# A two-layer decoder trunk on one core: weight differences, query-tile roots, paired transposes and halved loads are re-ordered

## The chip, the cores and the metric

The kernel runs on one core of a Trainium2 chip. The metric is the device time of one execution, in microseconds (us), as the median of several runs. A core has a matrix engine (TensorE; PE in the profile, with its weight loads shown apart as PEld), three elementwise engines (VectorE = DVE, ScalarE = ACT, GpSimd = POOL) and SyncE (SP), which here does little but issue DMA transfers, in the order of its queue. The engines run their own instruction streams in order and wait for each other by semaphores.

## The reference

The input is one sequence of 1024 positions of width 1024, all in 32-bit floats, with 256 memory tokens. There are two layers. Each normalises its input, multiplies it with one wide weight matrix, mixes the result over the positions, attends to the memory tokens, multiplies by a gate and projects back:

```python
for l in range(DEPTH):                       # 2
    h = rms_norm(x, norm_gain[l])
    cols = h @ w_in                          # mixer columns | memory queries | gate
    mix = dilated_mixer(...) if l % 2 == 0 else hgrn2_mixer(...)
    mem_out = memory_cross_attention(q_mem, mem, ...)
    y = concatenate([mix, mem_out]) * silu(gate)
    x = x + y @ w_out
```

The first layer's mixer has three groups of eight heads. Each group has its own q, k and v (1024 columns each), attends causally in a window of 128 keys gathered with a stride of 1, 4 or 16, with q and k normalised per head and rotated; the three outputs are merged per head by their softmax denominators. The second layer's mixer is a gated linear recurrence, done in chunks; its values are 1024 columns of the wide product.

## The kernel before

**Products in two parts.** A 32-bit product is made of three fast ones: each operand is split into a high part (a copy by ACT, `split_high`, `high_b`, written `h_` in the lists below) and a low part (the difference, by DVE, `split_low`, `low_b`, `l_`); PE adds high x high, high x low and low x high.

**Seven products instead of eight.** The nine q, k and v products of the first layer, and the v product of the second, are made in the 2 x 2 block scheme with seven block products, p = 0 to 6. The right-hand blocks of a product are raw weights (`11`, `21`, `12`, `22`, each in two halves of 512 KB) or differences of them, which `combine` makes on DVE: 12 - 11, 22 - 12, 22 - 11, 21 - 22. The products with p = 0 and 1 use the raw blocks 11 and 21. Each block product has four tiles, i = 0 to 3, and each tile is a step of twelve matmuls of 128 x 512. `step(k)` runs step k = 4 n + i of product n: the matmuls, then the emptying of the tile before, then `weights_ahead(n, i)`, which prepares the weights of the next block product: high parts at i = 0 and 1, low parts at i = 1 and 2, differences and loads by small tables. The variable `late` shifts the first three differences by one step; it is 0 in the first layer and 1 in the second.

**Tiles of q and k** of the first layer are normalised and rotated after their last product (DVE and POOL), then turned by PE six steps behind (`flip`, four 128 x 128 transposes into one bank of `pT`, which has two), copied out one step later by ACT (`spill_heads`) and stored to DRAM by a DMA on SP's queue (`qk_scr`). 96 such tiles are made, in runs of consecutive steps that start at an even step. After the last step the same function runs eight times more without matmuls, between matmuls for the memory tokens; two tiles of the memory are turned through `pT` there as well (`mem_turn`).

**The attention of the first layer** goes through twelve pairs (g, hp) of a group and two heads, in the order of `heads`, with eight steps m each. A step computes scores (L1537), turns an earlier step's weights (L1551), multiplies an earlier one with v (L1564, four steps after its scores), and fills PE with gate products while g is 2. After every second step the output goes through one of three `os` tiles to `o_scr` in DRAM, two stores of 128 KB; for g = 0 the three groups' outputs are merged instead, with the others loaded back (`og`). q, k and v of a pair, 1 MB each, are loaded ahead: `fetch_qk(at + 2)` at step 0, `fetch_v(at + 1)` at step 3. There are three rooms for q and k and two for v. For g = 1 these loads are already in two halves, for g = 0 and 2 each is one load. For g = 0, `fetch_v` also loads the statistics of the other groups. Only PE's order is written out here; a planner orders the other engines and SP's queue.

**The start of the second layer** has eight query tiles t (`project`, 24 matmuls each), whose matmuls hide other work: `slots[t]` lists the block sums of the 2 x 2 scheme for the left-hand side. `w_` adds high and low part to a whole block on POOL, `c_` combines blocks on DVE, `h_` and `l_` split them again. Beside them each step turns the query tile of two steps ago (L363), copies out the one of three steps ago (`spill_q`), and takes the root of the one before (`root_q`: a reduction and a scaling on DVE, a power on POOL, L1768 to L1770), then squares its own tile (`square_q`, two operations of ACT). Here PE, DVE, ACT and POOL all run in the order in which the code writes them (`pinned`). The seven-product scheme for v follows at once; the raw weights `21` (half 0) and `12` are loaded into room that the block sums leave.

Of the kernel before, what the change touches and what calls it, by code (L numbers as in the profile page):

```python
# [54 lines left out]
BEHIND = 6  # L55
# [48 lines left out]
def trunk_kernel(ctx, tc, x, mem, pos, norm_gain, w_in_a, q_gain_a, k_gain_a, qk_gain_t, w_out_a,  # L104
# [4 lines left out]
    LQ, SQ, WQ = Y, A, Y  # L109
# [689 lines left out]
    with ExitStack() as sa:  # L799
# [171 lines left out]
        def split_low(n, h):  # L971
            if n < 7 * len(groups):
                hi = highs.pop((n, h))
                lo = wpool.tile([128, 1024], F32R, name="wl")
                V.tensor_tensor(lo[:], source(n, h), hi.bitcast(F32), op=OP.subtract)  # L975
                split[n, h] = [t.rearrange("p (k n) -> p k n", k=2) for t in (hi, lo[:])]
# [4 lines left out]
        def weights_ahead(n, i):  # L981

            gi, p = divmod(n, 7)
            first, second = (1, 0) if p == 0 else (0, 1)
            sums_ = {(0, late): ("12", "12", "11", 0), (0, 1 + late): ("12", "12", "11", 1), (0, 2 + late): ("22", "22", "12", 0),
                     (1, 0): ("22", "22", "12", 1), (1, 3): ("11", "22", "11", 0), (2, 0): ("11", "22", "11", 1),
                     (2, 3): ("21", "21", "22", 0), (3, 0): ("21r", "21r", "22", 1)}
            if i in (0, 1):
                split_high(n + 1, (first, second)[i])
            if i in (1, 2):  # L990
                split_low(n + 1, (first, second)[i - 1])
            if (p, i) in sums_:
                out, a, b, h = sums_[p, i]
                combine(gi, out, a, b, h)
            for at, what in (((0, 2), ((0, "22", 1),)), ((2, 2), ((0, "21r", 1),)), ((2, 3), ((1, "11", 0),)),
                             ((3, 0), ((0, "22r", 0),)), ((3, 1), ((0, "22r", 1),)), ((4, 2), ((1, "11", 1),)),
                             ((4, 3), ((1, "12", 0), (1, "12", 1), (1, "21", 0))), ((5, 2), ((1, "22", 0),)),
                             ((5, 3), ((1, "21", 1),))):
                if at == (p, i):
                    for more_, b, h in what:  # L1000
                        load(gi + more_, b, h)
# [118 lines left out]
        late = 0  # L1120
# [4 lines left out]
        def step(k, fill=None):  # L1125

            n, i = divmod(k, 4)
            if k <= LAST and k not in sums_at:
                sums_at[k] = matmuls(k)
            spill_heads(k - 1 - BEHIND)  # L1130
            if k - 1 in sums_at:
                emptied(k - 1, sums_at.pop(k - 1))
            normed(k - 3)
            if k <= LAST:
                weights_ahead(n, i)
                if 3 < k < 26 and made_tables:
                    if next(tables, tables) is tables and made_tables:
                        made_tables.pop()()
                if i == 3 and n % 7 == 0 and groups[n // 7][0] != 2:
                    group_tables(*groups[n // 7])  # L1140
            if fill:
                fill()
            spread(k - 1)
            flip(k - BEHIND)

        wraws, W, gates = {}, {}, {}

# [233 lines left out]
        rooms_ = [None, None]  # L1381

        def fetch_qk(at):
            if at >= len(heads):
                return
            g, hp = heads[at]
            pool, n = (rooms_[1], 2) if at % 3 else (rooms_[0], 1)
            q, k = (pool.tile([128, 2, S], F32, name=name, bufs=n) for name in ("qT", "kT"))
            heads_at[g, hp] = q, k
            for i, t in ((1, k), (0, q)):  # L1390
                if g == 1:
                    src = qk_scr[i][g].rearrange("p h s -> p (h s)").rearrange("p (a h c) -> p a h c", a=2, c=512)
                    for a in range(2):
                        LQ.dma_start(t[:].rearrange("p h (a c) -> p a h c", a=2)[:, a], src[:, a, 2 * hp:2 * hp + 2])
                else:
                    LQ.dma_start(t[:], qk_scr[i][g][:, 2 * hp:2 * hp + 2])

        def fetch_v(at):
            if at >= len(heads):
                return  # L1400
            g, hp = heads[at]
            pool = rooms_[at % 2]
            v = pool.tile([128, NT, 256], F32, name="vv", bufs=1)
            src = v_scr[g][:, hp * 256:(hp + 1) * 256]
            if g == 0:
                LQ.dma_start(v[:], src.rearrange("(m p) c -> p m c", p=128))
            elif g == 1:
                src = src.rearrange("(a p b) c -> p a b c", a=2, b=4)
                for a in range(2):
                    LQ.dma_start(v[:, 4 * a:4 * a + 4], src[:, a])  # L1410
            else:
                LQ.dma_start(v[:], src.rearrange("(p m) c -> p m c", m=8))
            st = pool.tile([128, 128], F32, name="st", bufs=1)[:, 0:NG * NT * 4].rearrange("p (g m a h) -> p g m a h", g=NG, m=NT, a=2)
            if g == 0:
                for i in range(2):
                    LQ.dma_start(st[:, 1 + i].rearrange("p m a h -> p m (a h)"), st_scr[i, hp].rearrange("(m p) c -> p m c", p=128))
            heads_at[g, hp] += v, st

        def fetch(at):
            fetch_qk(at)  # L1420
            fetch_v(at)


        with ExitStack() as sm:
# [84 lines left out]
        if True:  # L1509
# [114 lines left out]

            fill = fillers()
            scored, turned, rest = [], [], []
            fetch_qk(1)
            for at, (g, hp) in enumerate(heads):
                for m in range(NT):
                    with pinned():  # L1630
                        new = (g, hp, m, *scores(g, hp, m))
# [13 lines left out]
                            {0: load_piece, 6: lambda: split_piece(0), 7: lambda: split_piece(1)}.get(m, lambda: None)()  # L1645
                        if g == 0 and m % 2:
                            others(hp, m - 1)
                        if m == 0:
                            fetch_qk(at + 2)
                        if m == 3:  # L1650
                            fetch_v(at + 1)
                    scored.append(new)
                    if old:
                        turned.append(old)
# [32 lines left out]
    with ExitStack() as sb:  # L1687
# [17 lines left out]
        with ExitStack() as s4:  # L1705
# [30 lines left out]
            def low_b(s_, j, e=V):  # L1736
# [14 lines left out]
                     5: ((w_, "21", 3), (w_, "22", 3), (c_, "s2", 2), (h_, "s2", 2), (l_, "s1", 2), (c_, "s4", 2), (h_, "s4", 2),  # L1751
                         (c_, "s3", 2), (h_, "s3", 2)),
                     6: ((w_, "11", 3), (l_, "s2", 2), (l_, "s4", 2), (l_, "s3", 2), (w_, "12", 3), (c_, "s1", 3), (h_, "s1", 3),
                         (c_, "s2", 3), (h_, "s2", 3)),
                     7: ((l_, "s1", 3), (c_, "s4", 3), (h_, "s4", 3), (c_, "s3", 3), (h_, "s3", 3), (l_, "s2", 3, G), (l_, "s4", 3),
                         (l_, "s3", 3, G))}
            normed_q, r_ = {}, {}

# [31 lines left out]
            for t in range(NT):  # L1790
                with pinned(E.PE, E.DVE, E.Activation, E.Pool):
                    ps = pss[t] if t < 2 else pp.tile([128, 512], F32, name="acc")
                    if t > 1:
                        project([ps[:]], [lhs_natural(order_q[t])], W)
                    turn_q(t - 2)
                    spill_q(t - 3)
                    root_q(t - 1)
                    run(slots[t])
                    square_q(t, ps[:])
            with pinned(E.PE, E.DVE, E.Activation, E.Pool):  # L1800
                root_q(NT - 1)
# [580 lines left out]
```

## Time and profile before

| | |
|---|---|
| median of 3 runs | 2069.23 us (2068.04 to 2072.08) |
| the profiled execution's own time | 2065.92 us |
| its span | 2064.0 us |
| PE busy | 2030.8 us, 98% |
| DVE, ACT, POOL busy | 1276.9, 889.1, 570.8 us |
| DMA, mean over the span | 143 GB/s |
| granted clock of PE, mean | 0.998 |

The span runs from the first to the last instruction of the program. Stages in the profile's own time: input and first gate 0 to 75 us, products of q, k and v to 800, memory tokens to 955, attention to about 1170, first output projection to 1340, query tiles of the second layer to 1390, v product and gates to 1500, memory attention, recurrence and the last projection to the end.

A row of a group of instructions gives line, engine, operation, tiles, how many, busy time, the mean of one in ns, then the engine's idle time before them and what ended it. A row of the timeline begins with its start and length in us; in brackets stands the idle time before it and the instruction that ended it. A row of PE's waits gives total us, how often, and the longest. Matmuls overlap, so that a row of 0.39 us can follow the one before by 0.23.

### The profile page before, as it was taken

The numbers are of one execution on the slowest core, as the hardware profiler recorded it, in microseconds if no ns is written. First come the engines' busy times: TensorE is split into PE (matmuls) and PEld (weight loads), VectorE is DVE, ScalarE is ACT, GpSimd is POOL, SyncE is SP. The second block draws the span as 40 slices with busy tenths as digits, with TensorE's granted clock in tenths as the row PEclk, the third lists the DMA queues.
The fourth block names the chain that finished last, engine by engine and source line by source line (L and its number), as shares of the span: only waits on it lengthen the run. The fifth ranks groups of instructions, "written<-read, shape, count | busy, mean of one in ns | idle before, by whom it ended". The sixth has DMA issues, their size and how long they took to land.

```text
span 2064.0 us, 29805 instructions
## 1 busy us (share of the span) xinstructions
PE 2030.8 (98%) x10641; PEld 1716.9 (83%) x10641; DVE 1276.9 (62%) x2540; ACT 889.1 (43%) x1678; POOL 570.8 (28%) x690
## 2 busy tenths in 40 slices
PE   7999999999999999999999999999999999999999
PEld 6888888888888887888898888877888888888887
DVE  7746866736767357555567454574554788876543
ACT  6435555633554345446666332253354323232220
POOL 4105765703755046131133200160031000000221
PEclk9999999999999999999999999999999999999999
DMA  6445999553544426527998474513354111213643
GB/s 228 133 133 103 95 142 132 108 168 90 120 119 134 152 72 195 172 70 264 313 333 265 153 250 153 170 61 132 125 173 142 32 51 45 79 42 102 236 133 112
DMA packets 431907, 295.59 MB, mean 143 GB/s; under 512 B 221568, under 2 KB 349840, under 8 KB 429712
## 3 DMA queue, kind: packets, MB, share of 16 engines
q1 hardware_dynamic: 418560, 276.91, 48.2%
q10 hardware_dynamic: 13200, 16.78, 2.2%
q8 instruction: 85, 1.39, 0.3%
q14 instruction: 62, 0.51, 0.1%
HBM read 202.28 MB, written 91.36 MB: 142 GB/s over the span
## 4 chain that ended last, share of the span: by engine, by line
PE 44%; DMA 4%; DVE 2%; ACT 2%; issue 1%; POOL 0%; SPq 0%; ACTq 0%; DVEq 0%
PE acc L662 4%; PE acc L663 4%; PE acc L664 4%; PE acc L558 4%; PE acc L556 4%; PE acc L557 4%; PE acc L1991 2%; DMA o_scr<-os 2%; PE s L2136 2%; PE pt L2136 2%; PE s L1537 1%; DMA og<-o_scr 1%; PE acc L1564 1%; PE po L1564 1%; PE pt L1551 1%; PE po L2270 1%
## 5 line engine op out<-in xcount | busy, mean ns | idle before, releaser
L174 ACT ACTIVATE wh<-raw 128x1024 fp32r<-128x1024 f32 x207 | 217.3, 1053 | 189.6 <-PE acc L557 60.0
L975 DVE TENSOR_TENSOR wl<-raw,wh 128x1024 fp32r<-128x1024 f32 x136 | 172.4, 1268 | 121.0 <-ACT wh L174 120.6
L1087 POOL TENSOR_TENSOR rr<-rv,nhalf 128x4 f32<-128x4 f32 x96 | 122.4, 1276 | 390.8 <-DVE rv L1085 390.2
L183 POOL TENSOR_TENSOR rr<-rv,nhalf 128x4 f32<-128x4 f32 (+1 forms) x46 | 43.1, 938 | 604.3 <-DVE rv L181 577.7
L662 PE MATMUL acc<-wh,yhi 128*128 128x512 f32 x360 | 142.7, 399 | 0.5 <-ACT yhi L174 0.5
L1042 PE MATMUL acc<-wh,hhi 128*128 128x512 f32 x360 | 141.9, 394 | 0.0
L663 PE MATMUL acc<-wl,yhi 128*128 128x512 f32 x360 | 141.1, 392 | 0.0
L1044 PE MATMUL acc<-wh,hlo 128*128 128x512 f32 x360 | 140.4, 390 | 0.0
L664 PE MATMUL acc<-wh,ylo 128*128 128x512 f32 x360 | 140.2, 394 | 0.0
L1043 PE MATMUL acc<-wl,hhi 128*128 128x512 f32 x360 | 140.2, 389 | 0.0
L556 PE MATMUL acc<-hhi,wh 128*128 128x512 f32 x320 | 128.7, 402 | 0.0
L557 PE MATMUL acc<-hlo,wh 128*128 128x512 f32 x320 | 127.6, 399 | 0.0
L558 PE MATMUL acc<-hhi,wl 128*128 128x512 f32 x320 | 127.4, 398 | 0.0
L236 DVE TENSOR_TENSOR wl<-raw,wh 128x1024 fp32r<-128x1024 f32 x62 | 76.6, 1239 | 66.4 <-ACT wh L174 60.8
L1542 ACT ACTIVATE pa<-pa,st 128x128 f32<-128x128 f32 (+1 forms) x192 | 84.5, 442 | 49.3 <-DVE st L1540 47.9
L979 DVE TENSOR_TENSOR raw<-raw 128x1024 f32<-128x1024 f32 x76 | 94.9, 1257 | 16.5 <-DMA raw<-in_w_in_a_dram 14.2
L674 DVE TENSOR_TENSOR x<-x,acc 128x512 f32<-128x512 f32 x62 | 42.1, 685 | 71.7 <-PE acc L664 71.7
L1540 DVE CUSTOM_DVE_ANT_0 pa<-s,masks 128x128 f32<-128x128 f32 (+1 forms) x192 | 59.6, 348 | 42.7 <-PE pt L1551 19.7
L1044 PEld LDWEIGHTS acc<-wh,hlo 128*128 128x128 f32 x360 | 67.6, 188 | 14.4
L1537 PE MATMUL s<-kT,qT 128*128 128x128 f32 (+1 forms) x384 | 78.2, 326 | 1.2 <-DVE st L1540 0.9
L662 PEld LDWEIGHTS acc<-wh,yhi 128*128 128x128 f32 x360 | 67.7, 188 | 14.0 <-ACT yhi L174 0.8
L664 PEld LDWEIGHTS acc<-wh,ylo 128*128 128x128 f32 x360 | 67.6, 188 | 13.9
(477 smaller groups left out, 5705.7 us busy)
## 6 DMA issues: line engine op xcount, KB each, us to landing
raw<-in_w_in_a_dram SPq DMA_DIRECT2D x109, 512.0 KB, 4.4
raw<-in_w_in_b_dram SPq DMA_DIRECT2D x43, 512.0 KB, 3.8
qk_scr<-m SPq DMA_DIRECT2D x48, 256.0 KB, 3.6
o_scr<-os SPq DMA_DIRECT2D x96, 128.0 KB, 5.8
kT<-qk_scr SPq DMA_DIRECT2D x8, 1024.0 KB, 6.3
qT<-qk_scr SPq DMA_DIRECT2D x8, 1024.0 KB, 9.0
vv<-v_scr SPq DMA_DIRECT2D x8, 1024.0 KB, 7.3
og<-o_scr SPq DMA_DIRECT2D x32, 256.0 KB, 5.5
```

What stands on the lines that cost most here:

```text
L174: A.activation(dst, src, AF.Copy)
L556: T.matmul(ps[:], wh[:, k, :], mh, start=k == 0, stop=False)
L557: T.matmul(ps[:], wh[:, k, :], ml, start=False, stop=False)
L558: T.matmul(ps[:], wl[:, k, :], mh, start=False, stop=k == 7)
L662: T.matmul(pss[ch][:], hi[:, k, :], wh[:, j, :], start=first and k == 0, stop=False)
L663: T.matmul(pss[ch][:], hi[:, k, :], wl[:, j, :], start=False, stop=False)
L664: T.matmul(pss[ch][:], lo[:, k, :], wh[:, j, :], start=False, stop=end and k == 3)
L975: V.tensor_tensor(lo[:], source(n, h), hi.bitcast(F32), op=OP.subtract)
L1042: T.matmul(flat, hi, wh, start=kt == 0 and p in (0, 1, 5), stop=False, **on)
L1043: T.matmul(flat, hi, wl, start=False, stop=False, **on)
L1044: T.matmul(flat, lo, wh, start=False, stop=kt == 3, **on)
L1087: G.tensor_tensor(r[:], sd[:], nhalf[:, :4], op=OP.pow)
```

## The change

Four edits:

1. `weights_ahead`: the first difference, 12 - 11 of half 0, is made at step i = 2 `late` of product 0, after that step's low part. With `late` = 1 this is step 2 instead of step 1, directly ahead of the difference of half 1; with `late` = 0 it stays in step 0.
2. `step`: tiles are turned in twos at every second step (the even one of a pair thus one step later), and copied out and stored in twos at the step after that.
3. `fetch_qk` and `fetch_v` become generators that issue one half of a load (512 KB) at a time; in the attention, steps 0, 1, 2 and 6 issue a half of k, k, q, q, steps 3 and 4 a half of v, step 5 the statistics.
4. Second layer: `root_q(t - 1)` stands behind the first three entries of `slots[t]` instead of ahead of all; the high part of `s2` of block row 3 moves from the end of slot 6 to the second place of slot 7.

```diff
-            sums_ = {(0, late): ("12", "12", "11", 0), (0, 1 + late): ("12", "12", "11", 1), (0, 2 + late): ("22", "22", "12", 0),
+            sums_ = {(0, 1 + late): ("12", "12", "11", 1), (0, 2 + late): ("22", "22", "12", 0),
...
+            if (p, i) == (0, 2 * late):
+                combine(gi, "12", "12", "11", 0)
             if (p, i) in sums_:
...
-            spill_heads(k - 1 - BEHIND)
+            if (k - BEHIND) % 2 == 0:
+                for t in (2, 1):
+                    spill_heads(k - t - BEHIND)
...
-            flip(k - BEHIND)
+            if (k - BEHIND) % 2:
+                for t in (1, 0):
+                    flip(k - t - BEHIND)
...
-                    for a in range(2):
-                        LQ.dma_start(t[:].rearrange("p h (a c) -> p a h c", a=2)[:, a], src[:, a, 2 * hp:2 * hp + 2])
-                else:
-                    LQ.dma_start(t[:], qk_scr[i][g][:, 2 * hp:2 * hp + 2])
+                    to = t[:].rearrange("p h (a c) -> p a h c", a=2)
+                for a in range(2):
+                    if g == 1:
+                        LQ.dma_start(to[:, a], src[:, a, 2 * hp:2 * hp + 2])
+                    else:
+                        LQ.dma_start(t[:, a], qk_scr[i][g][:, 2 * hp + a])
+                    yield
...
+            for a in range(2):
+                LQ.dma_start(v[:, 4 * a:4 * a + 4], src[:, a] if g == 1 else src[:, 4 * a:4 * a + 4])
+                yield
             if g == 0:
                 for i in range(2):
                     LQ.dma_start(st[:, 1 + i].rearrange("p m a h -> p m (a h)"), st_scr[i, hp].rearrange("(m p) c -> p m c", p=128))
...
             for at, (g, hp) in enumerate(heads):
+                qk, vs_ = fetch_qk(at + 2), fetch_v(at + 1)
                 for m in range(NT):
...
-                        if m == 0:
-                            fetch_qk(at + 2)
-                        if m == 3:
-                            fetch_v(at + 1)
+                        next(vs_ if 3 <= m < 6 else qk, None)
...
                      6: ((w_, "11", 3), (l_, "s2", 2), (l_, "s4", 2), (l_, "s3", 2), (w_, "12", 3), (c_, "s1", 3), (h_, "s1", 3),
-                         (c_, "s2", 3), (h_, "s2", 3)),
-                     7: ((l_, "s1", 3), (c_, "s4", 3), (h_, "s4", 3), (c_, "s3", 3), (h_, "s3", 3), (l_, "s2", 3, G), (l_, "s4", 3),
+                         (c_, "s2", 3)),
+                     7: ((l_, "s1", 3), (h_, "s2", 3), (c_, "s4", 3), (h_, "s4", 3), (c_, "s3", 3), (h_, "s3", 3), (l_, "s2", 3, G), (l_, "s4", 3),
                          (l_, "s3", 3, G))}
...
+                    run(slots[t][:3])
                     root_q(t - 1)
-                    run(slots[t])
+                    run(slots[t][3:])
```

More of the change, by code (lines that the diff above doesn't have):

```diff
@@ L1404, in fetch_v @@
             src = v_scr[g][:, hp * 256:(hp + 1) * 256]
[L1405 to L1412, printed above, removed]
-            st = pool.tile([128, 128], F32, name="st", bufs=1)[:, 0:NG * NT * 4].rearrange("p (g m a h) -> p g m a h", g=NG, m=NT, a=2)
+            st = pool.tile([128, 128], F32, name="st", bufs=1)[:, 0:NG * NT * 4].rearrange("p (g m a h) -> p g m a h", g=NG, m=NT, a=2)
+            heads_at[g, hp] += v, st
+            src = src.rearrange(("(m p) c -> p m c", "(a p b) c -> p a b c", "(p m) c -> p m c")[g], **({"p": 128}, {"a": 2, "b": 4}, {"m": 8})[g])
+            for a in range(2):
+                LQ.dma_start(v[:, 4 * a:4 * a + 4], src[:, a] if g == 1 else src[:, 4 * a:4 * a + 4])
+                yield
             if g == 0:
@@ L1416, in fetch_v @@
                     LQ.dma_start(st[:, 1 + i].rearrange("p m a h -> p m (a h)"), st_scr[i, hp].rearrange("(m p) c -> p m c", p=128))
-            heads_at[g, hp] += v, st
         def fetch(at):
-            fetch_qk(at)
-            fetch_v(at)
+            for _ in (*fetch_qk(at), *fetch_v(at)):
+                pass
         with ExitStack() as sm:
@@ L1626, in trunk_kernel @@
             scored, turned, rest = [], [], []
-            fetch_qk(1)
+            for _ in fetch_qk(1):
+                pass
             for at, (g, hp) in enumerate(heads):
+                qk, vs_ = fetch_qk(at + 2), fetch_v(at + 1)
                 for m in range(NT):
```

## The prediction, made before the change was timed

> **What bounds the kernel.** I read the page first, then who waited for whom on PE, then the windows of the stages that the diff touches, then their timelines.
>
> ```profile
> span 2064.0 us, 29805 instructions
> PE 2030.8 (98%) x10641; PEld 1716.9 (83%) x10641; DVE 1276.9 (62%) x2540; ACT 889.1 (43%) x1678; POOL 570.8 (28%) x690
> ```
>
> TensorE is busy for 98% of the span, and none of the edits takes work from it. So only what PE waits for, or runs slowly through, can be won. The list of PE's waits gives where (us in total, times, longest):
>
> ```profile
> PE po L1564 <- ACT os L174: 3.9, 2, 2.9
> ...
> PE s L1043 <- DVE wl L975: 1.9, 1, 1.9
> ...
> PE pt L363 <- ACT os L174: 1.7, 2, 1.1
> ...
> PE po L1564 <- DVE os L1616: 1.3, 2, 1.0
> ...
> PE pt L346 <- ACT u L1111: 0.3, 1, 0.3
> ```
>
> Lines 1564 (values of the attention), 1043 and 363 (first product and query tiles of the second layer) are next to edits. The windows (PE, PEld, DVE, ACT and POOL busy, granted clock, DMA share, GB/s) show the size of it:
>
> ```profile
> 75.00:800.00 725.00, 725.00 (x3367) 599.36 (x3366) 461.16 (x634) 345.92 (x460) 320.14 (x465) 1.00 0.58 124
> 970.00:980.00 10.00, 10.00 (x76) 9.29 (x75) 7.42 (x36) 7.70 (x30) 0.00 (x0) 1.00 1.03 385
> 1020.00:1030.00 10.00, 7.07 (x41) 6.21 (x40) 3.73 (x19) 4.49 (x15) 6.48 (x6) 0.83 0.92 267
> 1397.50:1401.00 3.50, 3.26 (x8) 2.58 (x9) 3.50 (x4) 1.01 (x1) 0.00 (x0) 0.55 0.06 23
> ```
>
> The first layer's products (75 to 800) have no idle PE at all. In two places the clock falls right after a wait: after the 2.9 us one near 1022 it is 0.83 over 10 us, which costs 10 x 0.17 = 1.7; after the 1.9 us one near 1396 it is 0.55 over 3.5 us, 3.5 x 0.45 = 1.6. A removed wait of that length is worth its clock too.
>
> **Part 1, first differences behind the low parts (second layer only).** With `late` = 1 the difference 12-11 of half 0 moves from step 1 to step 2, behind `split_low` of the second product's other half; in the first layer (`late` = 0) only its place in the code changes.
>
> ```profile
> 1392.07 1.06 ACT L174 ACTIVATE wh<-raw 128x1024 fp32r<-128x1024 f32 x1
> 1392.70 0.39 PE L1042 MATMUL po<-wh,hhi 128*128 128x512 f32 x1
> 1395.33 1.23 DVE L979 TENSOR_TENSOR raw<-raw 128x1024 f32<-128x1024 f32 x1 [2.38 <-DMA raw<-in_w_in_b_dram]
> 1395.42 0.39 PE L1042 MATMUL s<-wh,hhi 128*128 128x512 f32 x1
> 1396.47 1.22 DVE L975 TENSOR_TENSOR wl<-raw,wh 128x1024 fp32r<-128x1024 f32 x1
> 1397.61 3.49 DVE L979 TENSOR_TENSOR raw<-raw 128x1024 f32<-128x1024 f32 x3
> 1397.74 0.72 PE L1043 MATMUL s<-wl,hhi 128*128 128x512 f32 x1 [1.94 <-DVE wl L975]
> ```
>
> DVE stands 2.38 us for the raw weights, with the second product's low part queued behind; its high part was ready at 1392.07 + 1.06 = 1393.13. With the new order the low part runs 1393.2 to 1394.4, ahead of its use at 1395.42. The wait (1.9) and its clock (1.6) go: 3.5. Late next would be the differences: four of about 1.16 (3.49 / 3) from 1395.33 end near 1400, no later than now, as the low part in front of them has moved out of their way. A step of 12 matmuls is 1395.42 - 1392.70 = 2.72, 0.227 each; the third product starts four steps after the second, near 1405 to 1406. That slack hides the difference that waits one step longer, and excludes a loss; its DMAs stay where they are. Bounds: 0 (the raw weights of the low part itself bind) to 3.5; taken 3.5.
>
> **Part 2, roots amid the sums.** In the query tiles' steps DVE and POOL now do the first three block operations before the root of the tile before, and `h_ s2 3` moves from ACT's end of step 6 into step 7.
>
> ```profile
> 1378.81 3.20 POOL L1716 TENSOR_TENSOR b<-hhi,hlo 128x512 f32<-128x512 f32 x2
> 1378.48 0.68 DVE L1738 TENSOR_TENSOR s3lo<-b,s3hi 128x512 fp32r<-128x512 f32 x1
> 1379.08 1.78 DVE L1721 TENSOR_TENSOR b<-b,b 128x512 f32<-128x512 f32 x1
> 1382.59 0.63 ACT L174 ACTIVATE s2hi<-x 128x512 fp32r<-128x512 f32 x1 [1.07 <-DVE x L1724]
> 1384.41 0.69 DVE L1768 TENSOR_REDUCE rq<-sq 128x4 f32<-128x512 f32 x1 [1.85 <-ACT sq L1762]
> 1385.38 1.40 POOL L1770 TENSOR_TENSOR rq<-rq,nhalf 128x4 f32<-128x4 f32 x1 [3.37 <-DVE rq L1769]
> 1388.82 1.07 ACT L174 ACTIVATE os<-pt 128x512 f32<-128x512 f32 x2
> 1389.46 0.66 PE L363 MATMUL pt<-ident,qn 128*128 128x128 f32 x4 [1.13 <-ACT os L174]
> ```
>
> The three engines wait in a ring: DVE 1.85 for the square, POOL 3.37 for DVE, ACT 1.07 for DVE, until ACT's copy out of the transposes at 1388.82 is late and PE waits (1.7 in all at L363). In the new order the two block sums (3.20) no longer wait for the root, and ACT's copy and square stand in front of `s2hi`. The root itself goes past those sums on POOL; its result is read only when all tiles are done, so that delay is free. Following the last tiles: `x` is there at 1382.6 (ACT's row), two DVE operations of 0.6 follow, then reduce and scale (0.8) and the last difference, 1385.2; ACT's `s3hi`, copy and square of the last tile (0.6 each) end at 1387.0, so the copies start there instead of at 1388.82 and the first is done at 1387.6. PE comes for it at 1389.46 - 1.13 - (1.7 - 1.1) = 1387.7 and finds it just ready; allowing 0.3 for signals, 1.4 of the 1.7 goes. Bounds: -1.1 to 1.7; -1.1 is one more collision like that of L1721, 1.78 beside POOL's sum where the operation before it takes 0.68; taken 1.4, since POOL's sums then fall where DVE waits. The Trainium skill (SBUF — State Buffer, shared port pair) says that DVE with two SBUF inputs and GpSimd exclude each other for a whole instruction; the 1.78 agrees. By that rule alone the moved sums could take one DVE slot more in each step, and the part would bring nothing.
>
> **Part 3, flips in twos.** 96 transposes of four blocks become 48 bursts of eight.
>
> ```profile
> 565.46 0.60 PE L363 MATMUL pt<-ident,u 128*128 128x128 f32 x4
> ...
> 566.13 0.40 PE L1043 MATMUL s<-wl,hhi 128*128 128x512 f32 x1
> ...
> 568.67 0.60 PE L363 MATMUL pt<-ident,u 128*128 128x128 f32 x4
> ...
> 1342.36 1.03 PE L346 MATMUL pt<-ident,xn 128*128 128x128 f32 x8
> ...
> 1343.46 0.40 PE L293 MATMUL acc<-wl,hhi 128*128 128x512 f32 x1
> ```
>
> Four blocks to the second matmul after them: 566.13 - 565.46 = 0.67, less one matmul of 0.227, is 0.44. Eight: 1343.46 - 1342.36 - 0.227 = 0.87. A pair costs 0.87 for 0.88: nothing. A whole step with a flip is 568.67 - 565.46 = 3.21 against 2.72, so 0.49; if the further 0.05 is paid once per burst, 48 x 0.05 = 2.4 is won. Between 0 and 2.4 I take 1.0. ACT's two spills, and their two stores on SP, fall in one step, and both transposing banks are held until then. The step's other activations and loads queue behind by one spill, about 0.6; what they feed is used a product (four steps) later, which hides it. At the end of the layer one wait is added: the memory tile's transposes now meet two full banks, not one.
>
> ```profile
> 805.42 0.59 ACT L1111 ACTIVATE w<-pt 128x512 f32<-128x512 f32 x1
> 806.06 0.66 PE L346 MATMUL pt<-ident,raw 128*128 128x128 f32 x4 [1.58 <-ACT w L1111]
> ```
>
> The next tile's wait (0.3) falls away, as no flip stands before it. Net from -1.0 (1.58 shrinks to one copy of 0.59) to +2.2 (one copy of 0.59 more, and a drop of the clock, 1.6); taken 0.
>
> **Part 4, loads in halves.** Eight heads have 1 MB loads of k, q and v; these become 24 more loads, and all halves go out one per step instead of at steps 0 and 3. A k or q half goes out at steps 0, 1, 2 and 6, v at 3 and 4, the statistics (before at 3) at 5, used five steps later. All pass SP's queue among the `o_scr` stores.
>
> ```profile
> o_scr<-os SPq DMA_DIRECT2D x96, 128.0 KB, 5.8
> kT<-qk_scr SPq DMA_DIRECT2D x8, 1024.0 KB, 6.3
> ...
> kT<-qk_scr SPq DMA_DIRECT2D x8, 512.0 KB, 5.3
> ```
>
> ```profile
> 966.99 2.02 SPq L1394 DMA_DIRECT2D kT<-qk_scr  x2
> ```
>
> ```profile
> 1002.92 0.87 PE s L1537 x4
> 1004.45 0.87 PE s L1537 x4
> ```
>
> Two halves took SP 2.02 to issue here, 1.0 each: 24 more over a stage of some 180 us are hidden, since SP has no more than issues to do, except where a load lands late for it (last rival). PE waits for `po` because ACT and DVE have no free `os` tile: three tiles, one per two steps of 1.53, cover 9 us, of which the store takes 5.8 in the median after it gets its turn. 2 MB of k and q ahead of a store are 2.1 MB / 385 GB/s = 5.4 us; half a MB is 1.4. So up to 4 us come off a store's latency, more than the longest wait (2.9). To be won: 3.9 + 1.3 + 1.7 of clock = 6.9. But the DMA share is 1.03, and what a store gains a load loses. Bounds 0 and 6.9; I take two thirds, 4.6, nearer to the row of the latency than to that of the share.
>
> **Sum.** 3.5 + 1.4 + 1.0 + 0 + 4.6 = 10.5 us. The profiled execution took 2065.92 (span 2064.0), 3.3 under the median of 2069.23; so 2055.4 for its like, and **2058.7** as the median.
>
> **Rivals.**
> - The attention is bound by its bytes: a faster store only makes a load later, and part 4 brings nothing. For it: share 1.03 at 970. Against: PE was 10.00 of 10 there, so the loads were in time. 10.5 - 4.6 = 5.9: 2063.3.
> - The second layer's waits are handed on (the low part's raw weights land too late, part 2 collides), the end of layer one takes its +2.2, and the queues in the attention, which are planned and not pinned, gain only half: 1.0 + 2.3 - 2.2 = 1.1: 2068.1. The change then doesn't do what it says. For it: SP issues that load behind stores. Against: DVE's row names the other load.
> - Slower: halves land late. PE waits for `vv` at the start of heads.
>
> ```profile
> DMA to landing us min/median/max: 4.2/7.1/13.1
> ```
>
> v is asked for nine steps before its use, 9 x 1.53 = 13.8, and the slowest landing was 13.1; the second half goes out a step (1.53) later. From a landing over 12.3 PE waits; if four heads wait 2 us each with 1.7 of clock, 4 x 3.7 = 14.8, without part 4's 4.6: +14.8 - 5.9 = +8.9: 2078.1. Against: 512 KB lands in 5.3, not 6.3, and fewer bytes stand ahead. The Trainium skill (DMA: Bandwidth & Descriptors, Bandwidth) asks for 1 MiB or more in a DMA to pass 75% of peak, which speaks for this rival. The trace does not bear it out: the window at 970, in which the halves issued at 966.99 moved, has the 385 GB/s quoted.
>
> **Chances.** Forecast 0.50 (2053 to 2063), bytes 0.25, handed on 0.15, late halves 0.10. A measurement here tells 0.2%, 4.1 us, from no change. Faster (under 2065.1): nearly all of the first (0.48), 0.21 of the second, 0.05 of the third: 0.74. Slower: 0.09 of the last. The same: 0.17. The range 2050 to 2069: the low end is the forecast with every upper bound (3.5 + 1.7 + 2.4 + 1.0 + 6.9 = 15.5, 2053.7) and the runs' spread of 4; the high end holds the third case and leaves out the last.
>
> **What would show it.** Part 1: L1043 no longer waits for `wl`, the clock near 1396 stays at 1.00. Part 2: L363 waits under 0.5 for `os`. Part 3: rows of x8 at L363, and 75 to 800 about 1 us shorter. Part 4: `os` off the list of PE's waits, `o_scr` under 5 us to landing. Wrong if PE waits for `vv`, `kT` or `qT`, if L346 waits over 2.5, or if the stages that the diff doesn't touch change length.

## The result, and the profile after

The changed kernel takes 2057.91 us in the median of four runs (2055.26 to 2058.84), the kernel before 2069.55: ratio 0.9943, 95% interval 0.993 to 0.9956, so 11.6 us or 0.57% less. The forecast was 2058.7.

The head of the page of the changed kernel (lines of the file move by up to 10: 1537 is now 1543, 1564 is 1570, 1042 to 1044 are 1044 to 1046), whose profiled execution took 2058.84 us:

```profile
span 2057.0 us, 29832 instructions
PE 2026.7 (99%) x10641; PEld 1720.2 (84%) x10641; DVE 1276.9 (62%) x2540; ACT 887.1 (43%) x1678; POOL 569.1 (28%) x690
```

What PE waited for in the changed kernel (total us, times, longest):

```profile
PE po L1570 <- ACT os L174: 3.7, 2, 2.7
PE pt L346 <- ACT w L1113: 3.4, 1, 3.4
PE po L1570 <- DVE os L1622: 2.3, 1, 2.3
```

The waits of the second layer's start (the second product for `wl`, the query tiles for `os`) are gone from this list. The `os` waits of the attention are not: 3.7 + 2.3 = 6.0 us where there were 3.9 + 1.3. The wait of the memory tiles, line 346, grew from 1.6 to 3.4. The windows of the changed kernel (columns as in the prediction):

```profile
75.00:800.00 725.00, 725.00 (x3378) 603.50 (x3378) 461.00 (x636) 342.46 (x461) 323.21 (x470) 1.00 0.56 124
800.00:825.00 25.00, 21.59 (x103) 18.09 (x103) 13.25 (x23) 13.87 (x23) 7.17 (x13) 0.86 0.63 186
955.00:1110.00 155.00, 146.72 (x1062) 134.66 (x1062) 96.14 (x478) 104.69 (x387) 26.40 (x24) 0.99 1.00 332
1340.00:1400.00 60.00, 60.00 (x285) 49.72 (x284) 49.67 (x61) 31.63 (x52) 34.24 (x24) 1.00 0.27 88
```

and the same places in the kernel before, where they were not shown yet:

```profile
800.00:825.00 25.00, 23.11 (x121) 18.99 (x120) 14.43 (x25) 14.29 (x24) 9.79 (x18) 1.00 0.59 172
955.00:1110.00 155.00, 147.73 (x1064) 134.91 (x1063) 96.60 (x476) 104.19 (x387) 26.41 (x24) 0.99 1.00 332
1340.00:1400.00 60.00, 56.41 (x263) 45.80 (x262) 44.61 (x58) 29.84 (x51) 37.12 (x25) 0.98 0.23 80
```

Read the counts of matmuls behind PE's busy time. By 800 us the changed kernel has started 11 more (3378 against 3367); at 0.227 us each it is 2.5 us ahead. From 800 to 825 it starts 18 fewer and falls back. In the attention the two do the same work at the same 332 GB/s with the DMA engines full (share 1.00). At the start of the second layer PE is busy for 60.00 of 60, before for 56.41.

The stages end at matmuls that can be found in each trace by their line, so their lengths can be set side by side. The columns: first product matmul to the first of line 591; from there to the first of line 389 (where the memory tiles are turned); on to the first score; first score to the last matmul of line 292 (the attention and what is laid under its end); on to the last of line 662 of the first projection; on to the last matmul of the second layer's wide product; all after it. Times are in us. Kernels with more than one edit name their parts; the last five are the changed kernel with a further edit, told of below.

| kernel | products | memory tiles | to scores | attention | projection | second layer's product | rest |
|---|---|---|---|---|---|---|---|
| before | 729.3 | 16.9 | 140.4 | 233.8 | 145.4 | 130.35 | 599.8 |
| before, again | 729.3 | 17.3 | 140.3 | 237.5 | 145.8 | 128.35 | 599.8 |
| part 1 | 729.2 | 16.7 | 139.6 | 237.3 | 145.6 | 127.15 | 599.9 |
| part 2 | 729.2 | 16.6 | 138.7 | 236.3 | 145.2 | 124.45 | 599.5 |
| parts 1, 2 | 729.2 | 16.8 | 140.5 | 239.2 | 145.5 | 124.45 | 599.5 |
| part 3 | 726.7 | 19.6 | 138.4 | 235.2 | 146.3 | 130.43 | 600.0 |
| part 4 | 729.3 | 16.8 | 140.0 | 233.3 | 144.6 | 130.55 | 599.8 |
| parts 1, 2, 3 | 726.7 | 19.8 | 138.3 | 234.6 | 145.5 | 124.76 | 599.5 |
| changed (all) | 726.7 | 20.9 | 138.8 | 233.6 | 144.7 | 124.45 | 599.8 |
| memory tiles a step apart | 726.7 | 20.5 | 139.1 | 238.6 | 145.4 | 124.45 | 599.5 |
| single turns at the end | 726.7 | 21.8 | 139.1 | 234.8 | 144.7 | 124.45 | 599.5 |
| SP in written order | 726.7 | 20.1 | 139.3 | 232.4 | 145.2 | 124.45 | 600.0 |
| stores on ACT's queue | 726.7 | 19.8 | 139.1 | 255.3 | 144.9 | 124.45 | 599.9 |
| statistics in longer runs | 726.7 | 19.9 | 138.7 | 231.7 | 145.5 | 124.45 | 600.3 |

Two things stand out. The product stages repeat to 0.1 us from kernel to kernel, and so show each edit sharply; the attention does not (233.3 to 239.2 in the first eleven rows), and one profile of it proves little. And between the two profiles, before and changed, 7.0 us are found (2064.0 less 2057.0), not 11.6: the profiled execution of before was 3.6 under its median of 2069.55, that of the changed kernel 0.9 over its own.

### The profile page after: what moved, and what is told of

Its sections match the earlier page's. It is cut to its first block, busy times and chain, and to the rows that moved or that the text cites. A ratio compares the mean times of both kernels' runs of the same rounds, so it can differ in the third digit from the quotient of the medians.

```text
span 2057.0 us, 29832 instructions
## 1 busy us (share of the span) xinstructions
PE 2026.7 (99%) x10641; PEld 1720.2 (84%) x10641; DVE 1276.9 (62%) x2540; ACT 887.1 (43%) x1678; POOL 569.1 (28%) x690
## 4 chain that ended last, share of the span: by engine, by line
PE 50%; DMA 2%; ACT 1%; DVE 0%; issue 0%; POOL 0%; SPq 0%; ACTq 0%; DVEq 0%
PE acc L662 4%; PE acc L663 4%; PE acc L664 4%; PE acc L558 4%; PE acc L556 4%; PE acc L557 4%; PE s L1543 2%; PE acc L1997 2%; PE s L2142 2%; PE pt L2142 2%; PE acc L294 1%; PE acc L293 1%; PE acc L292 1%; PE pt L1557 1%; PE po L1570 1%; PE acc L1570 1%
## 5 line engine op out<-in xcount | busy, mean ns | idle before, releaser
L979 DVE TENSOR_TENSOR raw<-raw 128x1024 f32<-128x1024 f32 x76 | 96.5, 1278 | 20.1 <-DMA raw<-in_w_in_a_dram 19.8
```

## The experiments

Each was timed beside the kernel before. Ratios are to the kernel before, with 95% intervals; a difference in us is worked out from the ratio.

### One part alone, or two

Parts 1 and 2 alone (the hunks of `weights_ahead` and `slots`):

```diff
+            if (p, i) == (0, 2 * late):
+                combine(gi, "12", "12", "11", 0)
...
+                    run(slots[t][:3])
                     root_q(t - 1)
+                    run(slots[t][3:])
```

> Only the edits of the second layer (parts 1 and 2). My theory after the result: the profile of the changed kernel shows no wait and no fall of the clock between 1340 and 1400 (PE 60.00 of 60.00, before 56.41), so these two parts alone give about half of the 11.6 us by which the medians differ: 5 to 6 us under the kernel before, ratio 0.9973. The rival, that the attention's loads carry most of the gain as the prediction had it (4.6 of 10.5), would leave these parts the predicted 4.9, or less if they hand the wait on.

Measured: 2065.38 us, ratio 0.9982 (0.9973 to 0.9991), 3.7 us less. In the trace the second layer's product is 5.9 us shorter (130.35 to 124.45); the attention happened to be the longest of the first eleven rows.

Part 3 alone (tiles turned and copied out in twos):

```diff
-            flip(k - BEHIND)
+            if (k - BEHIND) % 2:
+                for t in (1, 0):
+                    flip(k - t - BEHIND)
```

> Only part 3, the transposes in twos. Theory: the products get about 1 to 2 us shorter, and the wait of the memory tile's transposes (3.4 us in the changed kernel, 1.6 before) with the fall of the clock behind it costs about 4, so that this part alone is 2 to 3 us slower: ratio 1.001. Rival (the prediction): 1.0 us faster, with a wait at L346 of under 2.5.

Measured: 2066.81 us, ratio 0.999 (0.9981 to 0.9999), 2.1 us less, so a little faster and not slower, with the memory tiles' wait at 3.3 us. The products win 2.6 (729.3 to 726.7), the memory tiles lose 2.7.

Part 4 alone (halved loads):

```diff
+                for a in range(2):
+                    if g == 1:
+                        LQ.dma_start(to[:, a], src[:, a, 2 * hp:2 * hp + 2])
+                    else:
+                        LQ.dma_start(t[:, a], qk_scr[i][g][:, 2 * hp + a])
+                    yield
```

> Only part 4, the loads in halves. Theory: the halves of k and q still leave SP back to back, because SP's order is planned and the loads wait for nothing, so PE's waits for a free os tile stay (5 to 6 us) and the time is that of the kernel before within 1 us. Rival (the prediction): 4.6 us faster, the waits for os gone.

Measured: 2065.06 us, ratio 0.9979 (0.9971 to 0.9988), 4.3 us less. But PE's waits for `os` are still in the list of this kernel:

```profile
PE po L1564 <- ACT os L174: 3.3, 2, 2.3
...
PE po L1564 <- DVE os L1616: 1.3, 2, 1.0
```

So the time fell as the prediction had it, while the waits stayed as the theory against it had it.

The three single figures make 3.7 + 2.1 + 4.3 = 10.1, the whole change 11.6; within the intervals they add up.

### The two parts of the second layer taken apart

Part 1 alone, and part 2 alone:

> The kernel before with part 1 alone (the first differences of the second layer behind the second product's low parts; roots and query tiles as before). Theory: the parts are separate, as the prediction has them. The wait of the second product's first matmul for its low part (1.9 us near 1396) and its slow clock go, 3.5 us; the ring of the query tiles stays, so the transposes of the query tiles still wait some 1.7 us for os. About 2066.0 against 2069.5, PE busy about 58 of 60 us in the window 1340 to 1400. Rival: the two places hang together, since the low part is late only because ACT and DVE leave the query tiles late; then part 1 alone gives the whole 3.7 to 5.8 us that both gave, and part 2 alone nearly nothing, or the other way round.

> The kernel before with part 2 alone (roots of the query tiles amid the block sums; the differences as before). Theory of the prediction: the transposes of the query tiles wait under 0.5 us for os, 1.4 us are won, the wait of the second product for its low part (1.9) stays: about 2068.1. Rival of the hanging together: the low part gets earlier too, its wait shrinks, and 3 to 5 us are won. Second rival: the moved sums collide on the shared port and nothing is won or up to 1.1 us lost.

Measured: part 1 2066.19 us, ratio 0.9981 (0.9973 to 0.999); part 2 2063.98 us, ratio 0.9969 (0.9957 to 0.9981). The windows at the place, part 1:

```profile
1340.00:1400.00 60.00, 58.31 (x277) 47.79 (x276) 44.96 (x57) 29.86 (x51) 40.45 (x27) 1.00 0.26 87
```

and part 2:

```profile
1340.00:1400.00 60.00, 60.00 (x286) 49.69 (x285) 49.52 (x62) 31.63 (x52) 36.39 (x25) 1.00 0.27 87
```

With part 1 the stage takes 127.15 us; the wait for `wl` is gone, the query tiles' 1.7 us for `os` stay, as forecast. With part 2 alone it takes 124.45, as with both: the wait for `wl` went too, though nothing of part 1 was done. The rival was right that the two stalls hang together. SP's queue shows how. In the kernel before (start, length, what is issued):

```profile
1389.43 0.81 SPq L1780 DMA_DIRECT2D qmb_scr<-os  x2
1390.33 0.95 SPq L955 DMA_DIRECT2D raw<-in_w_in_b_dram  x2
```

and with part 2 alone:

```profile
1382.96 4.26 SPq L955 DMA_DIRECT2D raw<-in_w_in_b_dram  x3
1387.31 0.89 SPq L1780 DMA_DIRECT2D qmb_scr<-os  x2
```

Before, DVE stands until 1395.33 for the first of the two loads at 1390.33, which goes out right behind the stores of the last query tiles. But the order of the queue is not what held it for most of the time. The load also needs its room, and the room is free only when POOL has read the last block sum out of it, for the last low part; the program has the load wait for that low part in both kernels. POOL in the kernel before:

```profile
1388.22 1.72 POOL L1738 TENSOR_TENSOR s3lo<-b,s3hi 128x512 fp32r<-128x512 f32 x1
```

and with part 2 alone, with the wait that SP's list shows for it:

```profile
1384.99 1.30 POOL L1738 TENSOR_TENSOR s3lo<-b,s3hi 128x512 fp32r<-128x512 f32 x1
```

```profile
SPq L955 <- POOL s3lo L1738: 2.9, 1, 2.9
```

Before, the low part ends at 1388.22 + 1.72 = 1389.94, and the stores hold the load for only 0.4 us more. With part 2 it ends at 1386.29, and the load, the second of the three in the row's 4.26 us, goes out at 1386.32. The second product's first two matmuls, in PE's timeline with part 2:

```profile
1394.32 0.39 PE L1042 MATMUL s<-wh,hhi 128*128 128x512 f32 x1
1394.54 0.39 PE L1043 MATMUL s<-wl,hhi 128*128 128x512 f32 x1
```

In the kernel before, the first of them was at 1395.42. So the weights go out 1394.32 - 1386.32 = 8.0 us ahead of it now, 1395.42 - 1390.33 = 5.1 before, and the matmul with `wl` follows after 0.22 us with no wait. Of these 2.9 us, some 2.5 are POOL's (its low part ends 8.0 us ahead of that matmul now, 5.5 before), and 0.4 are the order of loads and stores on SP. Which of part 2's two edits brings POOL's low part forward, the later root or the moved high part, isn't told apart, since both were made together.

### The memory tiles

The wait at line 346 grew with part 3 in every kernel that leaves the memory tiles' turns as they were (3.3 to 3.8 us). PE in the changed kernel:

```profile
800.29 1.03 PE L363 MATMUL pt<-ident,w 128*128 128x128 f32 x8
804.74 1.97 PE L346 MATMUL pt<-ident,raw 128*128 128x128 f32 x8 [3.41 <-ACT w L1113]
```

and ACT there:

```profile
799.20 0.72 ACT L221 ACTIVATE wh<-raw,tabs 128x512 fp32r<-128x512 f32 x1 [2.56 <-DMA raw<-in_w_mem_kv_dram]
...
800.35 1.93 ACT L221 ACTIVATE wh<-raw,tabs 128x512 fp32r<-128x512 f32 x3
802.30 1.28 ACT L519 ACT_TABLE_LOAD   x1
803.60 0.60 ACT L519 ACTIVATE os<-acc 128x512 f32<-128x512 f32 x1
804.09 1.08 ACT L1113 ACTIVATE w<-pt 128x512 f32<-128x512 f32 x2
```

The pair fills both banks at 800.29; ACT comes to empty them only after four weight splits, a table load and another copy, and empties both in a row at 804.09. The granted clock falls after the wait, in this window of the changed kernel to 0.60:

```profile
806.00:812.00 6.00, 6.00 (x23) 4.92 (x22) 1.39 (x2) 1.21 (x3) 1.99 (x6) 0.60 0.80 199
```

From 800 to 825 it is 0.86 (1.00 before), 25 x 0.14 = 3.5 us. In the first trial the memory's first tile is turned a step earlier:

```diff
-                if k in (3, 4):
-                    mts.append(mem_turn(k - 3))
+                if k in (2, 4):
+                    mts.append(mem_turn(k // 2 - 1))
```

> The changed kernel, with the memory tiles turned one step earlier and one step earlier than planned by the code (at the 2nd and 4th step after the products, where no pair of turned tiles stands directly before), so that both banks are free. Theory: the 3.4 us wait and the half clock behind it go, 4 to 5 us under the changed kernel, about 2053.5. Rival: the wait only moves to the turned pair behind the memory tile, and nothing is gained.

Measured: 2062.09 us, ratio 0.9961 (0.9949 to 0.9974); not better than the changed kernel (0.993 to 0.9956), rather some 4 us worse, though the two intervals overlap a little. PE's row there:

```profile
806.32 1.94 PE L363 MATMUL pt<-ident,w 128*128 128x128 f32 x8 [4.26 <-DVE s3lo L324]
```

The wait has only moved to the last pair of q and k tiles, which now stands behind the memory's. In the second trial the tiles behind the last product step are turned and copied out singly again:

```diff
-            if (k - BEHIND) % 2 == 0:
+            if k > LAST or (k - BEHIND) % 2 == 0:
...
+            if k > LAST:
+                flip(k - BEHIND)
+            elif (k - BEHIND) % 2:
```

> The changed kernel, but after the last product step the tiles are turned one at a time again, as in the kernel before; the pairs within the products stay. Theory: the pair that stands directly before the memory tile's transposes causes their 3.4 us wait and the half clock behind it; with single tiles it falls back to 1.5 to 1.9 us at full clock, and the time is 3 to 4 us under the changed kernel, about 2054.5. Rival: the wait comes from ACT's own work there (a table load and two other operations ahead of its copies) and stays near 3 us; no gain.

Measured: 2061.43 us, ratio 0.9963 (0.995 to 0.9975), no better than the change. The single turns do not bring the old 1.6 back; PE waits twice:

```profile
803.26 0.66 PE L346 MATMUL pt<-ident,raw 128*128 128x128 f32 x4 [1.88 <-ACT w L1113]
...
805.66 1.12 PE L346 MATMUL pt<-ident,raw 128*128 128x128 f32 x4 [1.74 <-ACT w L1113]
```

So the pair by itself does not make the wait. In all these kernels ACT's weight splits stand ahead of the copies that PE waits for, with the table load behind them, and the splits begin when a load of the memory's weights lands. In the kernel before that was hardly later than in the changed one:

```profile
799.81 1.34 ACT L221 ACTIVATE wh<-raw,tabs 128x512 fp32r<-128x512 f32 x2 [1.48 <-DMA raw<-in_w_mem_kv_dram]
```

With shorter products PE begins to wait some 3 us sooner (804.74 - 3.41 = 801.33, before 806.06 - 1.58 = 804.48), but ACT is done with its copies only 0.8 us sooner (805.17, before 806.01). The table shows the same: from the first product matmul to the first of line 389 it is 746.1 us on the mean of six kernels without part 3, and 746.7 of six with it and the memory tiles as they were. What the products win is lost here. This is read from the rows; no run moved that load.

### The halves in the attention

In the changed kernel SP still issues them back to back (SP's timeline):

```profile
1010.83 1.90 SPq L1423 DMA_DIRECT2D st<-st_scr  x2
1012.82 3.25 SPq L1403 DMA_DIRECT2D kT<-qk_scr  x2
1016.12 0.98 SPq L1403 DMA_DIRECT2D qT<-qk_scr  x2
1017.20 0.94 SPq L1590 DMA_DIRECT2D o_scr<-os  x2
```

The source asks for one half per step, but in this loop only PE's order is kept as written (`pinned()`), SP's is planned. The next kernel keeps SP's too:

```diff
-                    with pinned():
+                    with pinned(E.PE, E.SP):
```

> The changed kernel with SP's queue in the attention held to the order in which the code issues the loads and stores. Theory: the planner puts the four halves of k and q back to back (1012.8 to 1016.6 in the changed kernel) and ahead of stores that are ready, which undoes the spreading; in the code's order a store has one half ahead of it, PE's waits for os fall from 6.0 to under 3 us, and the time is 3 to 5 us under the changed kernel. Rival: the stage is bound by the bytes of its transfers (share 1.00 from 955 to 1110), and the waits only change their place; within 1 us of the changed kernel, or slower where SP now stands for a store that is not yet written.

Measured: 2058.8 us, ratio 0.9953 (0.994 to 0.9966), the same as the changed kernel within the intervals. SP now does what the prediction described:

```profile
1011.68 0.91 SPq L1590 DMA_DIRECT2D o_scr<-os  x2
1012.68 0.45 SPq L1403 DMA_DIRECT2D kT<-qk_scr  x1
1013.23 0.96 SPq L1590 DMA_DIRECT2D o_scr<-os  x2
```

and the wait of 3.7 for ACT's `os` is gone from PE's list; others came:

```profile
PE s L1543 <- issue: 2.6, 1, 2.6
...
PE po L1570 <- DVE os L1622: 1.4, 1, 1.4
...
PE pt L1557 <- DVE pts L176: 1.1, 1, 1.1
```

So spreading the halves does free the stores, and the freed stores are not what makes the time. Next, the stores of groups 1 and 2 go out on ACT's queue, past all of SP's loads:

```diff
-                    Y.dma_start(group_rows(o_scr[g][hp // 2], g, m - 1 + i)[:, hp % 2 * 256:hp % 2 * 256 + 256],
+                    SQ.dma_start(group_rows(o_scr[g][hp // 2], g, m - 1 + i)[:, hp % 2 * 256:hp % 2 * 256 + 256],
```

> The changed kernel with the o_scr stores of groups 1 and 2 issued on ACT's queue instead of SP's. Theory (order on SP's queue): these stores no longer stand behind loads, they land in 2 to 3 us instead of 5 to 6, and the waits for os that end with ACT (3.7 us, with the half clock behind the longest) go: 3 to 5 us faster than the changed kernel. Rival (bytes): the landing stays at 5 us, because the transfers share the same engines, and ACT's issue time (some 0.4 us a store, 64 of them) makes its weights late: same or slower.

Measured: 2080.23 us, ratio 1.005 (1.0035 to 1.0065), slower. These 64 stores land sooner on ACT's queue (line 1590; from issue to landing):

```profile
DMA to landing us min/median/max: 1.7/4.6/7.9
```

In the changed kernel the same 64 take:

```profile
DMA to landing us min/median/max: 2.0/5.6/9.4
```

PE's list in the kernel with the stores on ACT's queue shows the price, and ACT's list where it comes from:

```profile
PE pt L1557 <- ACT pa L1548: 14.4, 7, 4.5
```

```profile
ACT pa L1548 <- DMA o_scr<-os: 7.8, 2, 4.5
...
ACT pa L1548 <- DMA raw<-in_w_in_a_dram: 5.3, 1, 5.3
```

The stores stand between the exponentials (`pa`) that PE waits for. Issuing one takes ACT 0.33 us in the median; the long waits are those in which ACT, with a store next in its queue, stands until an earlier transfer has landed. The attention takes 255.3 us. At last the statistics' loads, the first row of SP's timeline above, which hold SP for 1.9 us ahead of the halves, are made of longer runs. The rows then come in another order, so this kernel leaves out the right merge of the three groups:

```diff
-... st_scr[i, hp].rearrange("(m p) c -> p m c", p=128))
+... st_scr[i, hp].rearrange("(p m) c -> p m c", p=128))
```

> The changed kernel, reading the statistics of groups 1 and 2 as one run of 128 bytes per partition instead of eight of 16; it takes them in another order of rows, so this part of the merge is left out in effect. Theory: the 2.7 us for which SP stands at 1012.8, right behind these two loads, come from their many short pieces; with whole runs SP doesn't stand there, the loads behind land some 2 us earlier, and the longest wait for os (2.7) falls under 1.5. Rival: SP stands there because the transfers ahead of it have not landed (share 0.97 to 1.00), whatever their pieces are, and nothing changes.

Measured: 2057.14 us, ratio 0.9941 (0.9927 to 0.9954), the same as the changed kernel. The longest wait for `os` was 2.2 us, not under 1.5 as the theory had it.

### All but the halves, and the kernel before again

> The changed kernel with the attention's loads whole, as before (parts 1, 2 and 3 alone). Theory: the halves are worth 4.3 us here as they were alone, though the profiles of the attention do not show it: 2062 to 2063 against the changed kernel's 2058. Rival: the halves are worth nothing in the mean, the 4.3 measured alone was a kernel's own offset, and this kernel takes 2058 to 2059 too. Second sign: the window 955 to 1110 moves 324 to 332 GB/s, like the changed kernel's; PE's waits for os there 5 us or more by the theory, 3 to 6 either way by the rival.

Measured: 2061.84 us, ratio 0.9957 (0.9944 to 0.9969), against the changed kernel's 0.9943 (0.993 to 0.9956). In place, the halves are worth 0.0014, some 3 us, but the intervals overlap; alone they were worth 4.3 (2.5 to 6.0). A gain of 2.5 to 4 us fits both. Where in the attention it lies, the traces do not say: seven executions with whole loads average 236.3 us in the table's column, four with halves in planned order (part 4, changed, memory tiles a step apart, single turns) 235.1, and either kind scatters by 5. The two kernels with halves and a further edit on SP (written order, longer runs) have the shortest, 232.4 and 231.7.

> The kernel before, unchanged, a second time: a control with a second profile. Theory: its time is the one of the other runs of before, ratio 1.000 within 0.001, and only its attention differs from the first profile, by up to 4 us more idle or slow PE between 955 and 1110, because the first profiled execution was 3.3 us under the median and everything else repeats to 0.3 us. Rival: the 3.3 us lie in the product stages or ahead of the first product, and the attention repeats to within 1 us.

Measured: 2069.67 us, ratio 0.9999 (0.999 to 1.0008). Its second profile, with a span of 2066.6 us, has 3.7 us more in the attention than the first. The rest doesn't all repeat, though: PE's wait for `wl` was shorter.

```profile
PE po L1564 <- ACT os L174: 4.8, 2, 3.8
...
PE s L1043 <- DVE wl L975: 1.5, 1, 1.5
```

After this 1.5 the clock stayed at 1.00, and the second layer's product took 128.35 for 130.35. Both sides of the expectation were partly right.

## Why the prediction was right, and where its steps were not

**Total.** 10.5 us were forecast off, 11.6 came. The time is right to 0.8 us; the terms are not all, and that the total comes so near is partly luck. The second layer gave more than forecast, the products gave 1.6 more and the memory tiles took 2.1 back, and these errors cancel.

**Part 1: 3.5 forecast, 3.2 alone (130.35 to 127.15; 1.2 against the second profile of before), nothing beside part 2.** The mechanism and size hold for the edit by itself: the low part runs ahead of the difference, wait and slow clock go. What failed is adding it to part 2. With part 2 the raw weights of the difference come in time, and there is nothing left for part 1 to win in the trace (124.45 with and without it).

**Part 2: 1.4 forecast, at most 1.7; 5.9 alone, 2.7 on top of part 1 (127.15 to 124.45).** The step that failed is the one that follows the loosened ring: it went on to ACT's copy and from there to PE at line 363, and to nothing else. On POOL it looked at the root alone ("that delay is free"). But the last two low parts stand behind a root in POOL's order, and the raw weights' load needs the room that the last of them reads. The rival "handed on" did name SP's queue ("SP issues that load behind stores"), but drew a loss from it; the queue's own share was 0.4 us. Together both parts were forecast at 4.9 and gave 5.9 in the trace. By the shared port of the Trainium skill (SBUF — State Buffer, SBUF: two separate sides), as the prediction applied it, the part would have brought nothing; the collision is there, in DVE's timeline with part 2:

```profile
1379.11 1.79 DVE L1738 TENSOR_TENSOR hlo<-b,hhi 128x512 fp32r<-128x512 f32 x1
```

while POOL's is

```profile
1378.64 1.70 POOL L1716 TENSOR_TENSOR b<-hhi,hlo 128x512 f32<-128x512 f32 x1
```

and over the query tiles eight of DVE's thirty block operations take more than 1.2 us, where six did before. The part brought 5.9 all the same.

**Part 3: 1.0 forecast, 2.6 in the products.** Taken was a value between 0 and 2.4; the reason behind the upper bound, 0.05 us per burst, is what came (2.6 / 45 = 0.06, as 45 of the 48 bursts lie ahead of the memory tiles). **The memory tiles: 0 forecast, bounds up to +2.2; +3.2** (mean of six kernels with part 3 and its memory tiles unmoved, single turns left out, 20.0, against 16.9 in six without). The prediction counted one more copy of 0.59 and 1.6 of clock. The step that failed is to take the wait from the number of copies: it did not read ACT's order ahead of them, where the table load of 1.28 and the weight splits stand, nor the load that the splits wait for, which landed only 0.6 us sooner (by the rows, 799.81 to 799.20) while the products ended 2.6 sooner. PE waits 3.4 us, and the clock falls after it; after the 1.58 of before it had stayed. The sign of the prediction's own test is met: "wrong if L346 waits over 2.5". Some 1.1 us come back before the scores (138.8 for 139.9 in the same kernels), by what isn't shown. The part's net in the traces is thus about -0.5, the timed one -2.1 (-0.2 to -3.9), the forecast -1.0.

**Part 4: 4.6 forecast, 4.3 timed alone, about 3 in place; the mechanism was wrong.** "All halves go out one per step" failed: SP's order is planned, and the planner puts them together again. "`os` off the list" failed with it: 6.0 us are on it. And where SP was made to spread them, most of these waits went (1.4 us were left) and the time did not. The stores land somewhat sooner: `o_scr` has a median of 5.8 in the kernel before and 5.1 in the changed one, which is not under 5, and the seven kernels with whole loads lie at 5.1 to 5.8 (part 2 alone at 5.1), those with halves in planned order at 4.9 to 5.2. What stays open is how the halves win what they win; the runs speak against the `os` waits as its main part. The rule of the Trainium skill (DMA: Bandwidth & Descriptors, Bandwidth) that asks for 1 MiB or more per DMA speaks against this part; the trace doesn't agree, as the attention moves the same 332 GB/s with 1 MB and with 512 KB loads.

**Rivals.** "Bound by its bytes" was right on its sign, a DMA share of 1.00 and 332 GB/s before and after, and wrong on its price: not nothing, but some 3 us. "Handed on" gave 2068.1 and is out; its end of layer one, +2.2, came about in size (+3.2 at the memory tiles, 1.1 of it back before the scores). "Late halves" is out: PE's list has no wait for `vv`, `kT` or `qT`.

**The sum's base.** 2065.92 - 10.5 = 2055.4 was the forecast for the profiled execution's like; the changed one took 2058.84. The correction to the median covered this: the second profile of before shows that the first had a short attention. Of the 11.6 us, then, the second layer gives 5.5 (mean of the four kernels with its old order, 129.9, to 124.45), the products 2.6 with 2.1 given back around the memory tiles, and the rest, by subtraction 5 to 6, is left to the attention and the projection, where no single profile can place it.

## What to carry to other kernels

When an edit loosens a ring of waits, follow it along every engine's order and on to the rooms that become free: a load waits for the last reader of its room as well as for its place in the queue, and the rows tell which ended last. Two stalls in a list of waits can have one cause and must not be summed. Time won ahead of a load that does not move can be lost again at that load. Before an edit of issue order is priced, find out whether that queue is kept as written or planned. Where stages repeat to 0.1 us and one does not, compare stage by stage, and judge the one that scatters by repeated times alone.

## What the runs showed that was not expected

The clock after a wait of PE. In the fourteen traces, PE had 46 waits of 1.2 us or more around the memory tiles, in the attention and at the second layer's start. Take the granted clock in the 3 us that begin 0.8 us after the start of the waiting instruction. After the fourteen waits up to 1.74 us it was 1.00, but for one that came 2.4 us after another wait of 1.88. Of the twelve from 1.88 to 2.58 us, eight were followed by 0.50 to 0.66 and four (2.21, 2.30, 2.33 and 2.58) by 1.00. All twenty from 2.75 us up were followed by 0.50 to 0.64. The Trainium skill (TensorE: Matmul & The Clock Gate, Part 1) gives one idle window of about 3.4 us as what halves the clock, a window that runs free of the kernel; the free window fits waits of one length that end either way, the length doesn't fit waits of 1.9 us. So a wait of 1.9 us mostly costs nearly as much again in clock (1.6 after the 1.94 of the kernel before), one of 1.7 standing alone did not, and a trim of a few tenths can be worth several times its size.

The spread of the attention. With the DMA engines full it took 233.8 and 237.5 us in two executions of one and the same kernel, while the products around it repeated to 0.1 us.
